# A macaron RWKV-7 block in split fp32: more Strassen-like quads in the down and output projections, and a planner that lists more of the transfers

## The chip, the cores and the metric

One core of a Trainium2 chip runs the whole block; everything below is one launch. The metric is device time in microseconds, the median of three runs: 2014.39 us before the change (2014.39 to 2014.5). The profiled execution, a run of its own, took 2014.53 us; its span, from the first instruction to the last, is 2012.8 us.

## The reference, cut to what matters

All arrays are fp32; 256 tokens, model width 2048, feed-forward width 5632.

```python
def _hybrid_mixer(u, w_in, ...):
    p = u @ w_in
    z_a, z_b, g_a, g_b = jnp.split(p, IN_SPLITS, axis=-1)
    y_a = _rwkv7_branch(z_a, ...) @ w_proj_a      # a scan over the tokens, 16 heads of 64
    y_b = _pool_branch(z_b, pool_w, pool_scale) @ w_proj_b
    m = jax.nn.sigmoid(g_a) * y_a + jax.nn.sigmoid(g_b) * y_b
    return m @ w_out

def reference(x, ...):
    f = _swiglu(_rmsnorm(h, ln_ffn1_pre[l]), ffn1_gate[l], ffn1_up[l], ffn1_down[l])
    h = h + MACARON_WEIGHT * _rmsnorm(f, ln_ffn1_post[l])
    mx = _hybrid_mixer(_rmsnorm(h, ln_mix_pre[l]), ...)
    h = h + _rmsnorm(mx, ln_mix_post[l])
    f = _swiglu(_rmsnorm(h, ln_ffn2_pre[l]), ffn2_gate[l], ffn2_up[l], ffn2_down[l])
    h = h + MACARON_WEIGHT * _rmsnorm(f, ln_ffn2_post[l])
```

## The kernel before

**Splitting.** Every fp32 operand of a matmul is split into a high and a low part of type fp32r, and a product is three matmuls (`mm3`, lines 271 to 275): high by high, low by high, high by low. The high part of a weight is a cast on ACT, the low part a subtraction on DVE (the "low" below). A weight tile holds two blocks of 128 rows by 512 columns. A tile is either one of a small ring (`w32` for the fp32 data, four buffers; `wH`, `wL`, five each) or one of 33 general units (`kH`, `kL`, and in some places `w32`).

**Pairs and quads.** `seven` (line 458) computes two column blocks of 512 at once, called f and l. A letter of its order string is one step. `f` or `l` is a plain pair: two k blocks, two token halves, three matmuls each, so 12 matmuls and one low of 1024 columns. `q` is a quad: two k blocks of both column blocks by seven products instead of eight, so 21 matmuls where an f and an l would need 24. For it DVE makes sums of weights (`t13`, `t24`) and three lows of 1024 and one of 512 columns, and the activations need sums of their own (`sums`, line 381). A capital letter is a pair whose low part is made without DVE (`feed_add`, line 304): ACT writes the negated high part, and an accumulating DMA, issued on POOL, adds the fp32 data.

**Stages.** A feed-forward block runs gate and up in column blocks of 512 (`ffn`, line 847; blocks 2 to 10 by `seven` with the orders of `FAST`), turns the result with DVE transposes and small POOL DMAs (`carry`, line 770), and then runs `post` (line 996): two column pairs of down with the orders of `DOWN`. The mixer's output projection uses `post` with `OUT`: a plain block, one pair by `seven`, a plain block. The last 16 k blocks of the last pair are done one token half after the other (`TRAIL`).

**The order of the work.** In the feed-forward blocks and the projections the PE order is written down in sequence, and every other operation is a job with a duration, a due time and its dependences. `play` (line 168) walks through time and hands out the jobs of ACT (A), DVE (V), POOL (G) and the weight transfers on SP (D), always the ready one with the earliest due time; what comes out is the fixed instruction order of each engine. On the chip nothing is reordered: an engine that waits holds up all that is queued behind it.

**The RWKV chain.** In the mixer PE alone has a written order. `chain(hf)`, for the two halves of the heads, yields the time of matmuls that shall stand between its steps, and `weave` puts that much of other work there (`fill`: the remaining input projections, and last `pair_g`, the first half of `w_proj_a` for two column blocks). `FILL` and `FILB` are two of these times, ahead of the first pA and the first pB of each half. The last steps of a half are the matmuls pY (scan output), pg (gate) and 64 small transposes pT; from pT and pg DVE makes the half's output y in two parts by eight scalar_tensor_tensor operations (lines 1767, 1769), ACT casts the high parts `yH` (1771), and DVE subtracts the low parts `yL` (1772). `w_proj_a` over the second half of y comes right behind in PE's order.

**The head.** SP first loads the transposed x and the first gate weights, then `cols`, then the four row tiles of x (lines 1806 to 1809), from which ACT takes the sums of squares.

## Time and profile before

| | |
|---|---|
| median of three runs | 2014.39 us |
| the profiled execution | 2014.53 us, span 2012.8 us, TensorE clock 0.998 |
| PE busy | 1997.0 us (99%), 9936 matmuls |
| DVE busy | 1764.8 us (88%) |
| ACT, POOL busy | 1200.2 us (60%), 339.8 us (17%) |
| HBM | 202 GB/s over the span |

PE is busy nearly all the time, but a matmul's recorded end is modelled, and the records overlap; what a matmul costs is the distance from start to start. The windows of 50 us say how close the other engines are: DVE is busy between 48.7 and 50.0 of 50 us from 150 to 450 us, in the gate and up blocks of the first feed-forward, 112.68 of 115 us in the first pair of the first down, and much less in the mixer.

### The profile page before, as it was taken

To read this page: it belongs to the slowest core of one execution; us is meant where nothing else is said; L and a number is where in the kernel's file an instruction comes from. 1 tells how busy PE (TensorE), PEld (TensorE's weight loads), DVE (VectorE), ACT (ScalarE), POOL (GpSimd) and SP (SyncE) were. 2 spreads that over 40 slices of the span, in tenths; PEclk is the share of its full clock that TensorE was granted. 3 is DMA by queue.
4 is the path that set the end of the run, shared out by engine and by line. 5 is a ranking of instruction groups with operands and counts; after the bars stand their busy time and mean duration, and the time that the engine had idled before them with its cause. 6 is when DMAs were issued, how large, how long until landed. Compare 5 with 4: busy or idle time off the path is not lost.

```text
span 2012.8 us, 28601 instructions
## 1 busy us (share of the span) xinstructions
PE 1997.0 (99%) x9936; PEld 1651.9 (82%) x9936; DVE 1764.8 (88%) x2362; ACT 1200.2 (60%) x1599; POOL 339.8 (17%) x689
## 2 busy tenths in 40 slices
PE   9999999999999999999999999999999999999997
PEld 7888888888888888888788788888888888888886
DVE  6999999999998857789689678679999999999885
ACT  7556666566655656775575444565556655756553
POOL 0131112211000113403220120002211131110000
PEclk9999999999999999999999999999999999999999
DMA  9777777766667777757466567766777877666674
GB/s 331 235 217 230 230 242 222 236 185 211 216 205 255 238 203 211 211 176 214 141 182 183 160 218 240 254 219 180 220 228 225 256 218 231 195 215 209 206 258 142
DMA packets 230305, 435.09 MB, mean 216 GB/s; under 512 B 25104, under 2 KB 28688, under 8 KB 230160
## 3 DMA queue, kind: packets, MB, share of 16 engines
q1 hardware_dynamic: 205008, 387.18, 59.9%
q0 software_dynamic: 24864, 45.95, 8.4%
q8 instruction: 78, 1.28, 0.3%
q14 instruction: 67, 0.55, 0.1%
q10 hardware_dynamic: 288, 0.14, 0.0%
HBM read 398.79 MB, written 8.39 MB: 202 GB/s over the span
## 4 chain that ended last, share of the span: by engine, by line
PE 97%; DVE 1%; issue 1%; ACT 1%; DMA 0%; SPq 0%; POOL 0%; DVEq 0%; POOLq 0%; ACTq 0%
PE mm L273 27%; PE mm L275 26%; PE mm L274 26%; PE ms L275 5%; PE ms L274 5%; PE ms L273 5%; PE pA L1596 0%; PE tr L750 0%; DMA w<-in_ffn_gate_dram 0%; PE mc L732 0%; DVE fg L1052 0%; PE pU L1692 0%; DVE wL L298 0%; DVE xL L759 0%; PE pSa L1704 0%
## 5 line engine op out<-in xcount | busy, mean ns | idle before, releaser
L273 PE MATMUL mm<-wH,xH 128*128 128x512 f32 (+1 forms) x1711 | 668.8, 391 | 0.0
L274 PE MATMUL mm<-wL,xH 128*128 128x512 f32 (+1 forms) x1711 | 663.2, 388 | 0.8 <-DVE wL L250 0.8
L275 PE MATMUL mm<-wH,xL 128*128 128x512 f32 (+1 forms) x1711 | 663.4, 388 | 0.3 <-DVE xL L759 0.3
L275 PEld LDWEIGHTS mm<-wH,xL 128*128 128x128 f32 x1711 | 321.2, 188 | 66.8 <-DVE xL L759 0.7
L273 PEld LDWEIGHTS mm<-wH,xH 128*128 128x128 f32 x1711 | 321.3, 188 | 66.3 <-ACT wH L249 0.3
L274 PEld LDWEIGHTS mm<-wL,xH 128*128 128x128 f32 x1711 | 321.5, 188 | 64.6 <-DVE wL L250 1.1
L292 ACT CAST wH<-w 128x1024 fp32r<-128x1024 f32 x251 | 262.6, 1054 | 174.8 <-PE mm L275 122.9
L298 DVE TENSOR_TENSOR wL<-w,wH 128x1024 fp32r<-128x1024 f32 x251 | 301.3, 1218 | 58.3 <-ACT wH L292 56.7
L530 ACT CAST wH<-t 128x1024 fp32r<-128x1024 f32 x163 | 171.8, 1054 | 194.5 <-DVE t L515 69.6
L250 DVE TENSOR_TENSOR wL<-w,wH 128x1024 fp32r<-128x1024 f32 (+2 forms) x159 | 188.2, 1192 | 74.4 <-ACT wH L249 73.0
L781 POOL DMA_DIRECT2D x<-T x352 | 173.3, 511 | 434.4 <-DVE T L768 238.0
L249 ACT CAST wH<-w 128x1024 fp32r<-128x1024 f32 (+2 forms) x159 | 162.7, 1027 | 135.6 <-PE mm L275 113.6
L534 DVE TENSOR_TENSOR wL<-t,wH 128x1024 fp32r<-128x1024 f32 x163 | 196.1, 1216 | 17.3 <-ACT wH L530 17.0
L530 ACT CAST wH<-w 128x1024 fp32r<-128x1024 f32 (+1 forms) x161 | 132.9, 826 | 120.7 <-PE mm L275 68.8
L273 PE MATMUL mm<-kH,xH 128*128 128x512 f32 x449 | 175.5, 391 | 0.0
L275 PE MATMUL mm<-kH,xL 128*128 128x512 f32 x449 | 174.9, 389 | 0.0
L274 PE MATMUL mm<-kL,xH 128*128 128x512 f32 x449 | 174.7, 389 | 0.0
L534 DVE TENSOR_TENSOR wL<-w,wH 128x1024 fp32r<-128x1024 f32 (+1 forms) x161 | 151.1, 938 | 1.1 <-ACT wH L530 1.0
L515 DVE TENSOR_TENSOR t<-w,w 128x1024 f32<-128x1024 f32 x104 | 126.5, 1217 | 6.5 <-DMA w<-in_ffn_down_dram 2.7
L298 DVE TENSOR_TENSOR kL<-w,kH 128x1024 fp32r<-128x1024 f32 x95 | 113.6, 1216 | 6.3 <-ACT kH L292 6.0
L292 ACT CAST kH<-w 128x1024 fp32r<-128x1024 f32 x95 | 98.1, 1048 | 19.5 <-DMA w<-in_ffn_gate_dram 9.3
L275 PEld LDWEIGHTS mm<-kH,xL 128*128 128x128 f32 x449 | 84.3, 188 | 18.0 <-DVE xL L759 0.5
(377 smaller groups left out, 2895.6 us busy)
## 6 DMA issues: line engine op xcount, KB each, us to landing
w<-in_w_in_dram SPq DMA_DIRECT2D x128, 512.0 KB, 4.2
w<-in_ffn_down_dram SPq DMA_DIRECT2D x116, 512.0 KB, 4.7
w<-in_ffn_up_dram SPq DMA_DIRECT2D x104, 512.0 KB, 5.0
w<-in_ffn_gate_dram SPq DMA_DIRECT2D x103, 512.0 KB, 6.1
w<-in_ffn_gate_dram SPq DMA_DIRECT2D x146, 256.0 KB, 4.1
w<-in_ffn_up_dram SPq DMA_DIRECT2D x144, 256.0 KB, 4.1
w<-in_ffn_down_dram SPq DMA_DIRECT2D x120, 256.0 KB, 4.2
w<-in_w_out_dram SPq DMA_DIRECT2D x28, 512.0 KB, 5.9
```

Source lines behind the costliest of these rows:

```text
L249: s.nc.scalar.copy(vH, v)
L250: s.nc.vector.tensor_tensor(out=vL, in0=v, in1=vH.bitcast(F32), op=ALU.subtract)
L273: nc.tensor.matmul(ps, aH, bH, start=start, stop=False)
L274: nc.tensor.matmul(ps, aH, bL, start=False, stop=False)
L275: nc.tensor.matmul(ps, aL, bH, start=False, stop=stop)
L292: s.nc.scalar.copy(b["H"][:, :m], b["t"][:, :m])
L298: s.nc.vector.tensor_tensor(out=b["L"][:, :m], in0=b["t"][:, :m], in1=b["H"][:, :m].bitcast(F32), op=ALU.subtract)
L515: V.tensor_tensor(out=v["t13"], in0=v["a"], in1=v["b0"].to_broadcast([P, 2, 512]), op=ALU.subtract)
L530: nc.scalar.copy(x[n_][0], v[n_])
L534: V.tensor_tensor(out=L, in0=v[n_], in1=H.bitcast(F32), op=ALU.subtract)
L781: nc.gpsimd.dma_start(out=x[0][q * 32:q * 32 + 32, i], in_=src[i * 32:i * 32 + 32, q])
```

## The change

The order strings change. The first pair of down gets eight quads instead of seven and one capital `L`; in all four strings the quads are mixed in among the pairs where they stood in rising density before. The output's pair gets four quads instead of two, and three capital letters in front. `FAST` for blocks 2 and 3 gets a second capital letter and another order. `FILL` goes from 19.5 to 20.5 and `FILB` from 5 to 6. The planner's transfer lag goes from 2.4 to 2.8, and `moved` adds empty jobs to its D list for transfers that POOL issues (carries, norm weights, reloads, mixer tiles, spills), so that it plans weights around them. The four row tiles of x move from the head into the planned list, with due times 0, 2, 4, 6. Units that hold fp32 weights are named `uw` instead of `w32`. `silu_in` and `times_in` get forms for blocks 0 and 1 that no order uses here (`SECOND` is empty).

```diff
-FILL = 19.5
-FILB = 5
+FILL = 20.5
+FILB = 6
-LAG = dict(P=0.2, A=0.18, V=0.16, G=0.2, D=2.4, N=0.0)
+LAG = dict(P=0.2, A=0.18, V=0.16, G=0.2, D=2.8, N=0.0)
-DOWN = ((0, "fffffffffqffffqfflqlllqllqllqllqlllll", 0),
+DOWN = ((0, "ffllfLlllqqffllfqfqllqfffffqllqfqfll", 0),
-OUT = ((0, "", 0), (1, "fffffqflqlllll", 0), (3, "", TRAIL))
+OUT = ((0, "", 0), (1, "LFLqqfqqflfl", 0), (3, "", TRAIL))
...
+    def moved(s, dur, due, *deps):
+        for d in deps:
+            s.job("D", dur, lambda: None, due, (d,))
...
         ms = [s.job("G", 0.49, lambda i=i, q=q: move(i, q), t, turned, lag=4.0) for i, q in iq]
+        s.moved(0.15, t, *ms)
...
-                s.job("G", 0.55, lambda: nc.gpsimd.dma_start(
-                    out=hsp[i, h, :, c * 512:c * 512 + 512], in_=ap), t + 9, (node,))
+                s.moved(0.9, t + 9, s.job("G", 0.55, lambda: nc.gpsimd.dma_start(
+                    out=hsp[i, h, :, c * 512:c * 512 + 512], in_=ap), t + 9, (node,)))
...
-                for h in range(2):
-                    for c in range(2):
-                        nc.sync.dma_start(out=xs[h][c], in_=x[0, h * P:h * P + P,
-                                                             c * 1024:c * 1024 + 1024])
...
+                    if c % 2 == 0:
+                        t = ROWS[2 * h + c // 2]
+                        d = s.job("D", 1.75, lambda h=h, c=c // 2: nc.sync.dma_start(
+                            out=xs[h][c], in_=x[0, h * P:h * P + P, c * 1024:c * 1024 + 1024]), t)
```

In the built programs PE has 12 instruction rows fewer, all of them 128x512 matmuls (8328 become 8316).

The longer `FILL` and `FILB` take fill from what stood behind the chain. First PE at the end of the second half's chain, before: pT, then `w_proj_a` over the first half of y (yH_3729, yL_3730), in groups of three matmuls; the fence shows the first two groups and the last, and behind it the first that reads the second half (yH_3731, yL_3732).

```order
L1763 MATMUL pT_4515_11525<-ident_78,R_3716_6723 64x64 x16
L273 MATMUL mm_4516_11548<-wH_4508_11488,yH_3729_6752 128x512
L274 MATMUL mm_4516_11548<-wL_4509_11489,yH_3729_6752 128x512
L275 MATMUL mm_4516_11548<-wH_4508_11488,yL_3730_6753 128x512
L273 MATMUL mm_4513_11498<-wH_4508_11488,yH_3729_6752 128x512
...
L273 MATMUL mm_4516_11548<-wH_4511_11494,yH_3729_6752 128x512
L274 MATMUL mm_4516_11548<-wL_4512_11495,yH_3729_6752 128x512
L275 MATMUL mm_4516_11548<-wH_4511_11494,yL_3730_6753 128x512
L273 MATMUL mm_4503_11442<-wH_7139_11624,yH_3731_6754 128x512
L274 MATMUL mm_4503_11442<-wL_7140_11625,yH_3731_6754 128x512
L275 MATMUL mm_4503_11442<-wH_7139_11624,yL_3732_6755 128x512
```

The same place after the change; the second half of y is yH_3948, yL_3949 there.

```order
L1788 MATMUL pT_4733_11559<-ident_78,R_3933_6738 64x64 x16
L281 MATMUL mm_4731_11517<-wH_4728_11509,yH_3946_6767 128x512
L282 MATMUL mm_4731_11517<-wL_4729_11510,yH_3946_6767 128x512
L283 MATMUL mm_4731_11517<-wH_4728_11509,yL_3947_6768 128x512
L281 MATMUL mm_4715_11428<-wH_7621_11639,yH_3948_6769 128x512
L282 MATMUL mm_4715_11428<-wL_7622_11640,yH_3948_6769 128x512
L283 MATMUL mm_4715_11428<-wH_7621_11639,yL_3949_6770 128x512
L281 MATMUL mm_4716_11432<-wH_7621_11639,yH_3948_6769 128x512
```

Seven groups of three stood between pT and the first use of the second half; one stands there now.

DVE at the same place, before: the lows of the second half's first three weights, then the eight operations on pT and pg with the first yL, then the fourth weight's low (wL_7147, from w32_7133), then the second yL.

```order
L298 TENSOR_TENSOR wL_7142_11628<-w32_7131_11608,wH_7141_11627 128x1024
L298 TENSOR_TENSOR wL_7144_11632<-w32_7132_11610,wH_7143_11631 128x1024
L1767 SCALAR_TENSOR_TENSOR R_3719_6726<-pT_4514_11502,cols_90,R_3719_6726 128x256 x2
L1769 SCALAR_TENSOR_TENSOR R_3719_6726<-R_3719_6726,cols_90,pg_4505_11450 128x256 x2
L1767 SCALAR_TENSOR_TENSOR R_3719_6726<-pT_4515_11525,cols_90,R_3719_6726 128x256 x2
L1769 SCALAR_TENSOR_TENSOR R_3719_6726<-R_3719_6726,cols_90,pg_4506_11459 128x256
L1772 TENSOR_TENSOR yL_3732_6755<-R_3719_6726,yH_3731_6754 128x512
L1769 SCALAR_TENSOR_TENSOR R_3719_6726<-R_3719_6726,cols_90,pg_4506_11459 128x256
L298 TENSOR_TENSOR wL_7147_11650<-w32_7133_11612,wH_7146_11649 128x1024
L1772 TENSOR_TENSOR yL_3732_6755<-R_3719_6726,yH_3731_6754 128x512
```

After, with wL_7628, from w32_7615, as the fourth weight's low:

```order
L306 TENSOR_TENSOR wL_7626_11647<-w32_7614_11625,wH_7625_11646 128x1024
L306 TENSOR_TENSOR wL_7628_11663<-w32_7615_11627,wH_7627_11662 128x1024
L1792 SCALAR_TENSOR_TENSOR R_3936_6741<-pT_4732_11536,cols_90,R_3936_6741 128x256 x2
L1794 SCALAR_TENSOR_TENSOR R_3936_6741<-R_3936_6741,cols_90,pg_4722_11483 128x256 x2
L1792 SCALAR_TENSOR_TENSOR R_3936_6741<-pT_4733_11559,cols_90,R_3936_6741 128x256 x2
L1794 SCALAR_TENSOR_TENSOR R_3936_6741<-R_3936_6741,cols_90,pg_4723_11492 128x256
L1797 TENSOR_TENSOR yL_3949_6770<-R_3936_6741,yH_3948_6769 128x512
L1794 SCALAR_TENSOR_TENSOR R_3936_6741<-R_3936_6741,cols_90,pg_4723_11492 128x256
L306 TENSOR_TENSOR wL_7631_11669<-uw_7616_11629,wH_7630_11668 128x1024
L306 TENSOR_TENSOR kL_7633_11673<-uw_7617_11631,kH_7632_11672 128x1024
L1797 TENSOR_TENSOR yL_3949_6770<-R_3936_6741,yH_3948_6769 128x512
```

The fourth weight's low has moved ahead of the whole y calculation, and two further lows, one before, stand between the two yL. ACT's casts of these weights moved with them.

POOL at the start of the output projection, before: the last mixer tile, the carry of the gated sum, the norm weights, the reload of the residual.

```order
L1339 DMA mb_7156_11680<-msp_6756 128x1024
L781 DMA sga_4305_10300<-T1_7164_11724 32x256 x16
L1011 DMA gb_4626_11571<-in_ln_mix_post_dram 128x1024
L1011 DMA gb_4627_11572<-in_ln_mix_post_dram 128x1024
L1830 DMA h1_2300_426<-hsp_131 128x1024
```

After, with the accumulating DMAs of the three capital letters:

```order
L1364 DMA mb_7636_11692<-msp_6771 128x1024
L789 DMA sga_4522_10315<-T1_7642_11719 32x256 x16
L1034 DMA gb_4863_11586<-in_ln_mix_post_dram 128x1024
L330 DMA wL_7689_11962<-uw_7674_11883 128x1024
L330 DMA wL_7697_12005<-w32_7680_11912 128x1024
L330 DMA kL_7707_12058<-w32_7690_11964 128x1024
L1034 DMA gb_4864_11587<-in_ln_mix_post_dram 128x1024
```

Three transfers are added to this stretch of POOL's queue, behind the carry and one load of norm weights.

More of the change, by code (lines that the diff above doesn't have):

```diff
@@ L864, in f @@
                     sig[h] = get()
[L865 to L866 removed]
+                    nc.scalar.activation(out=sig[h], in_=sig[h], func=AF.Silu, scale=r[h])
+                sj[h] = s.job("A", 0.59, f, t, (*deps, b < 2 and uj[h]))
                 return sj[h]
@@ L1024, in ev @@
                         s.job("N", 0, None, 0, (a,))
-                        s.job("G", 0.0, reload, t, (a,))
+                        g = s.job("G", 2.0, reload, t, (a,))
+                        for i in range(4):
+                            s.moved(1.75, t + 4 * i, g)
                     def some():
```

43 lines of the change are left out of this document (29 added, 14 removed).

## The prediction

> **What bounds the kernel now.** I read the page first (busy time, then the chain that ended last), then PE's waits, then the chain piece by piece at both ends and around the RWKV steps, then windows by stage.
>
> ```profile
> PE 1997.0 (99%) x9936; PEld 1651.9 (82%) x9936; DVE 1764.8 (88%) x2362; ACT 1200.2 (60%) x1599; POOL 339.8 (17%) x689
> PE 97%; DVE 1%; issue 1%; ACT 1%; DMA 0%; SPq 0%; POOL 0%; DVEq 0%; POOLq 0%; ACTq 0%
> ```
>
> The chain runs through PE for 97% of the span. PE's whole list of waits (engine, line, what it waited for, us in total, times, longest):
>
> ```profile
> PE warm L649 <- POOL ident masks.py:199: 1.7, 1, 1.7
> PE mm L274 <- DVE wL L250: 0.8, 1, 0.8
> PE pS L1712 <- ACT R L1706: 0.7, 1, 0.7
> PE mm L275 <- DVE xL L759: 0.3, 1, 0.3
> ```
>
> Without the warm-up that is 1.8 us in the whole run. The matmuls follow each other at the engine's own pace, here in the chain near the end (start, us, what), 20 matmuls between the two rows:
>
> ```profile
> 1984.91 0.23 PE mm L273
> ...
> 1989.44 0.24 PE mm L275
> ```
>
> 4.53 us for 20 is 0.2265 us each. So the kernel is as long as its matmuls, plus some 7 us in front and 11 behind the last one, which the change leaves as they are. A gain comes from fewer matmuls, or from the 1.8 us; a loss comes from any new wait of PE. I looked for those.
>
> **The matmuls.** A quad needs 21 matmuls where two pairs need 24. One more in the first pair of each down, two more in the output's pair: 4 x 3 = 12 fewer, as in the built programs. 12 x 0.2265 = 2.72 us, all on the path. The Trainium skill (TensorE: Matmul & The Clock Gate, Back-to-back issue gap) gives a sustained 131 ns for matmuls of 512 columns beside their weight loads; 12 x 0.131 would be an estimated 1.57 us, and the sum below 2014.6; the trace, with 0.2265, disagrees, and decides.
>
> **DVE in down.** Windows by stage (stretch, length, then PE, PEld, DVE, ACT, POOL busy, clock, DMA share, GB/s): the first pair of the first down, its second pair, the two halves of the output projection, the first pair of the second down; then the DVE groups of the first stretch.
>
> ```profile
> 464.00:579.00 115.00, 115.00 (x509) 95.27 (x508) 112.68 (x143) 69.97 (x89) 8.39 (x17) 1.00 0.66 215
> 579.00:693.00 114.00, 114.00 (x513) 94.46 (x512) 96.44 (x114) 66.81 (x89) 5.48 (x10) 1.00 0.70 230
> 1225.00:1275.00 50.00, 50.00 (x226) 41.53 (x225) 37.68 (x42) 23.79 (x29) 0.54 (x1) 1.00 0.56 176
> 1275.00:1320.00 45.00, 45.00 (x208) 37.27 (x207) 37.05 (x62) 27.99 (x58) 7.13 (x13) 1.00 0.81 276
> 1764.00:1879.00 115.00, 115.00 (x509) 95.27 (x508) 111.48 (x143) 67.03 (x83) 8.39 (x17) 1.00 0.67 216
> ```
> ```profile
> L298 DVE TENSOR_TENSOR wL<-w,wH 128x1024 fp32r<-128x1024 f32 x31 | 37.0, 1219 | 1.0 <-ACT wH L292 0.8
> L519 DVE TENSOR_TENSOR t<-w,t 128x512 f32<-128x512 f32 x8 | 5.5, 683 | 0.0
> L405 DVE TENSOR_TENSOR sf<-x 128x256 f32<-128x256 f32 x4 | 1.7, 418 | 0.0
> ```
>
> A quad costs DVE four operations of 1.219 (t13 and three lows) and three of 0.683: 6.93 us. The first pair of down gains a quad and loses three plain lows (30 before, 27 now): 6.93 - 3.66 = 3.27 us more. DVE has 115 - 112.68 = 2.32 us idle there in the first down, 3.52 in the second, and 17.6 in the pair that follows. The second capital letter in blocks 2 and 3 takes 2 x 1.219 = 2.44 us off DVE before it. I take nothing for it, as the excess, 3.27 - 2.32 = 0.95, is less than that; the bounds are 0 and 0.95 in the first down and 0 in the second. The quads that now stand early in the string shift DVE's work within the stage; below 0 it can't go, since PE has no wait there to lose.
>
> **DVE and POOL in the output's pair.** Plain lows 12 become 5 (8.5 us less), two quads add 13.9, their activation sums four operations of 0.418 and two like 1.219, 4.1: together 9.5 us more, against 12.3 + 7.95 us of DVE idle in the two windows. Nothing. The nine further accumulating DMAs (one in each of blocks 2 and 3 and in down, per feed-forward, and three at the output) land some 7 us after their issue:
>
> ```profile
> kL<-w POOLq DMA_DIRECT2D x9, 512.0 KB, 6.7
> ```
>
> The planner starts them 9 us ahead of use, and none of the 18 of before is in PE's list. I take nothing; if POOL's queue (carry in front) holds one up, the cost is between 0 and one whole landing, 6.7.
>
> **The head and the planner's entries.** The rows of x now start behind three weights on SP instead of ahead of them. Weights come earlier, the row statistics later; they are needed for the gate's evacuation, whose banks PE wants again only after the 96 matmuls of up, 21.7 us later. Nothing. The empty jobs and the lag issue nothing; they only change the order of ACT, DVE, POOL and SP.
>
> **The end of the RWKV chain.** This is where I expect a new wait. Each half of the chain takes some 2 us more fill (1 + 1 by the constants), and for the second half that fill was what hid the calculation of y: seven groups of three matmuls, 4.8 us, stood between pT and the first use of the second half of y; one group, about 0.9 us with the slower first matmul, is left. The first half's end shows how long y takes when DVE is free (chain, then ACT, then DVE by the timeline):
>
> ```profile
> 1013.31 2.01 PE pT L1763 x64
> 1015.32 0.43 PE mm L273
> 1015.75 0.23 PE mm L274
> ```
> ```profile
> 1016.12 0.62 ACT L1771 CAST yH<-R 128x512 fp32r<-128x512 f32 x1 [0.25 <-DVE R L1769]
> ```
> ```profile
> 1014.43 0.88 DVE L1767 SCALAR_TENSOR_TENSOR R<-pT,cols,R 128x256 f32<-128x256 f32 x2 [0.25 <-PE pT L1763]
> ...
> 1017.18 0.68 DVE L1772 TENSOR_TENSOR yL<-R,yH 128x512 fp32r<-128x512 f32 x1
> 1017.79 0.47 DVE L1769 SCALAR_TENSOR_TENSOR R<-R,cols,pg 128x256 f32<-128x256 f32 x1
> 1018.67 1.22 DVE L250 TENSOR_TENSOR wL<-w,wH 128x1024 fp32r<-128x1024 f32 x1 [0.42 <-ACT wH L249]
> 1019.82 0.68 DVE L1772 TENSOR_TENSOR yL<-R,yH 128x512 fp32r<-128x512 f32 x1
> ```
>
> From pT's end at 1015.32 (call it T) yH is done at T + 1.42, the first yL at T + 2.54, the second at T + 5.18, with one low in between. Now: PE has its one group done at T + 0.89 and waits for yH, 0.53 us; two matmuls later, at T + 1.88, it waits for yL until T + 2.54, 0.66 us. The next three groups take it to T + 4.8, and the third matmul of the fifth group, at T + 5.3, needs the second yL. There two lows stand in between instead of one: without the wait of 0.42 that is T + 5.85, with it T + 6.3, so 0.57 to 1.0 us. In all 1.8 us (1.76 to 2.2). Queued behind PE's wait is the rest of `w_proj_a`, which everything later waits for, so it counts in full. The second half's own end in the trace of before says the same: pT ends at 1186.69, and the first yL is done at 1189.74, 3.05 us later.
>
> ```profile
> 1184.68 2.01 PE pT L1763 x64
> ```
> ```profile
> 1189.05 0.69 DVE L1772 TENSOR_TENSOR yL<-R,yH 128x512 fp32r<-128x512 f32 x1
> ```
>
> **The sum.** -2.72 + 1.8 = -0.9 us. From the profiled execution, 2014.53 (span 2012.8), that is 2013.6; the median lies 0.14 lower, so 2013.5. About 0.2%, 4.0 us, is what a measurement of this kernel can tell from no change.
>
> **The rivals.** *The fourth weight is late, and the kernel is slower.* The fourth weight of `w_proj_a`'s second half has its low now ahead of all of y on DVE, and its cast ahead of yH on ACT. In the trace of before ACT waited for just this weight:
>
> ```profile
> 1189.22 1.05 ACT L292 CAST wH<-w 128x1024 fp32r<-128x1024 f32 x1 [0.61 <-DMA w<-in_w_proj_a_dram]
> ```
> ```profile
> 1174.80 5.30 SPq L235 DMA_DIRECT2D w<-in_w_proj_a_dram  x4
> ```
> ```profile
> 1175.06 1.06 POOL L1339 DMA_DIRECT2D mb<-msp  x2 [2.02 <-issue]
> ```
> ```profile
> DMA to landing us min/median/max: 3.7/8.0/11.9
> ```
>
> It landed at 1189.2, T + 2.5, the last of the four issues that began at 1174.80, beside the mixer tiles that POOL loads; landing there took up to 11.9 us where 3.7 is possible (all weights from 1165 to 1215). The Trainium skill has a rule for this (DMA: Bandwidth & Descriptors, Issuing engines are not separate DMA queues): transfers of SP, ACT and POOL run on the same 16 engines and interleave; by it the mixer tiles delay the weight, and the trace agrees. Cast and low take 1.05 + 1.22, and y would otherwise start at T - 0.89, so each us that it lands after T - 3.2 delays PE by one. The change frees its buffer some 5 us sooner, as PE uses up the first half's weights earlier; issued 5 us sooner it lands near T - 2.5 or before, a delay of 0.7 at most, and with a median landing of 8.0 at none. If it stays in the queue behind the mixer tiles, it comes as late as before: 5.7 us more, 2019.2; halfway, 2016.4. The kernel is slower than before from 0.9 us on, that is from a landing at T - 2.3. Chance 0.25, with 2016 as its middle.
>
> *y is hidden anyway*: 2014.39 - 2.72 = 2011.7. For it, DVE's work before pT may be so short that y starts earlier; against it, y can't start before pT, and PE has 0.9 us of work left. Chance 0.17.
>
> *DVE falls behind in down, or an accumulating DMA is late*: 0.95 from the first down, up to 6.7 from one landing, on top of the 1.8: 2014.5 to 2020. The windows speak against the first, the list of waits against the second. Chance 0.09.
>
> *The change doesn't do what it says*: 12 matmuls are gone in any case, but the planner's entries could remove PE's remaining waits, and with y hidden that gives 2014.39 - 2.72 - 1.8 = 2009.9. Of the 1.8, 0.8 is in the head before anything that moved. Chance 0.04.
>
> **How the numbers follow.** The forecast, 2013.5, has 0.45. The range takes in y hidden at its lower end (2011.7, less 0.2 for a lost wait) and the late weight beyond halfway at its upper: 2011.5 to 2017.4; outside are the full lateness, a late DMA and the lost waits, about 0.15 to 0.2. Faster by over 0.2% needs 2010.4 or less: only the last rival, 0.04. Slower by over 0.2% needs 2018.4: the late weight in full, 0.06, a late DMA or several small waits, 0.05: 0.11. The rest, 0.85, is within 0.2%.
>
> **What would show it.** In the changed profile: PE 12 matmuls shorter, the same 0.2265; in PE's waits new entries of about 0.5 on ACT yH, 0.7 and 0.6 on DVE yL, right behind the second pT, and no DMA named in ACT's wait before them. The forecast is wrong if these are missing (then 2011.7), if DVE's first operation on pT starts after pT's end (the late weight), or if PE waits for a low in down or for a `kL` in the output's pair.

## The result, and the profile after

The changed kernel is slower: 2020.33 us median (2018.58 to 2025.64, 7 runs) against 2014.88 for the kernel before (2014.39 to 2015.11, 7 runs); the recorded ratio is 1.0031, with a 95% interval of 1.0021 to 1.0042 (it is not the quotient of the two medians, which is 1.0027). The forecast was 2013.5, its range ended at 2017.4. The profiled execution took 2020.33 us, span 2018.5.

The page's lines on the engines and on the chain, and then PE's whole list of waits (engine, line, what it waited for, us in total, times, longest), of the changed kernel:

```profile
PE 1997.3 (99%) x9924; PEld 1646.4 (82%) x9924; DVE 1775.9 (88%) x2379; ACT 1211.2 (60%) x1617; POOL 349.7 (17%) x698
PE 91%; DVE 4%; DMA 2%; issue 2%; ACT 0%; POOL 0%; SPq 0%; DVEq 0%; POOLq 0%; ACTq 0%
```
```profile
PE warm L657 <- POOL ident masks.py:199: 1.7, 1, 1.7
PE tr L758 <- DVE sga L1377: 1.6, 1, 1.6
PE mm L282 <- DVE wL L258: 1.0, 2, 0.8
PE pU L1717 <- DVE R L1742: 0.8, 1, 0.8
PE mm L281 <- ACT wH L257: 0.7, 1, 0.7
PE mm L283 <- DVE yL L1797: 0.6, 2, 0.4
PE mm L281 <- ACT yH L1796: 0.6, 1, 0.6
PE mm L281 <- DVE u L581: 0.5, 1, 0.5
PE ms L282 <- DVE wL L542: 0.2, 1, 0.2
```

PE runs twelve matmuls less, and yet its busy time has not fallen, so the busy time does not show what was lost. The chain shows it better: DVE and the DMAs hold 6% of it, where PE had 97% before and has 91% now. The waits on yH and yL are the forecast ones; those on sga, on pU, on `u` (a gate operation of the first feed-forward) and on the lows of down (wL, line 542) are not.

**Where the time went.** The instructions that are no 128x512 matmuls (transposes and the small matmuls of the mixer) are the same 1608 in both programs, so the start of the same one can be compared. "Matmuls" is how many more 128x512 matmuls stand ahead of it after the change, and "net" is the difference of the starts less 0.2265 us for each.

| mark on PE | before, us | after, us | matmuls | net, us |
|---|---|---|---|---|
| transposes of the row statistics (head) | 57.71 | 58.30 | 0 | 0.59 |
| first transposes behind the first down | 686.98 | 688.64 | -3 | 2.34 |
| pg of the second half | 1177.82 | 1182.49 | +15 | 1.27 |
| first transposes of the gated sum (sga) | 1207.84 | 1210.52 | -3 | 3.35 |
| their second part | 1219.62 | 1224.02 | -3 | 5.08 |
| last matmul | 2000.16 | 2005.07 | -12 | 7.63 |
| end of the span | 2012.8 | 2018.5 | -12 | 8.4 |

So 8.4 us were lost and 2.7 gained: 0.6 at the head, 1.75 in the first feed-forward with its down, 2.08 at the end of the RWKV chain, 1.73 at the second part of the sga transposes, 2.55 in what follows (nearly all in the second down), 0.7 behind the last matmul; the mixer up to pg gave 1.07 back, for a reason that stays open. Only the third of these had been forecast. The list of waits shows little of what the downs lost: in the second one the largest idle time of PE is 0.18 us, and 2.2 of the 2.55 us are fourteen delays of 0.10 to 0.34 us from one start to the next.

**The end of the chain.** DVE there (start, length, instruction), from the first operation on pT to the second yL:

```profile
1190.48 0.88 DVE L1792 SCALAR_TENSOR_TENSOR R<-pT,cols,R 128x256 f32<-128x256 f32 x2 [0.78 <-PE pT L1788]
...
1193.23 0.69 DVE L1797 TENSOR_TENSOR yL<-R,yH 128x512 fp32r<-128x512 f32 x1
...
1194.22 1.22 DVE L306 TENSOR_TENSOR wL<-uw,wH 128x1024 fp32r<-128x1024 f32 x1
1195.36 1.22 DVE L306 TENSOR_TENSOR kL<-uw,kH 128x1024 fp32r<-128x1024 f32 x1
1196.49 0.69 DVE L1797 TENSOR_TENSOR yL<-R,yH 128x512 fp32r<-128x512 f32 x1
```

DVE's first operation waits 0.78 us for pT itself, so the fourth weight was not late. PE, which has one group of matmuls left, then waits for yH and both yL; the two lows between the yL are those of the order.

**The sga transposes.** DVE at the second part of the gated sum, before and then after:

```profile
1213.77 1.30 DVE L1349 TENSOR_TENSOR sga<-mm,sga 128x512 f32<-128x512 f32 x2
1214.98 0.68 DVE L1352 TENSOR_TENSOR sga<-sga,mb 128x512 f32<-128x512 f32 x1
1218.21 1.29 DVE L807 TENSOR_TENSOR xL<-sga,xH 128x512 fp32r<-128x512 f32 x2 [2.55 <-ACT xH L803]
1219.42 0.69 DVE L1352 TENSOR_TENSOR sga<-sga,mb 128x512 f32<-128x512 f32 x1
```
```profile
1220.78 1.30 DVE L816 TENSOR_TENSOR xL<-sga,xH 128x512 fp32r<-128x512 f32 x2 [3.48 <-ACT xH L812]
1221.99 1.28 DVE L1374 TENSOR_TENSOR sga<-mm,sga 128x512 f32<-128x512 f32 x2
1223.19 1.28 DVE L1377 TENSOR_TENSOR sga<-sga,mb 128x512 f32<-128x512 f32 x2
```

xL is the low of the carried first part; it waits for ACT's xH, and that for the last of the carry's DMAs (landed at 1220.0). Before, three of the four gate operations (those on sga) were done ahead of that wait; now all four are queued behind it, and PE's transposes need the last of them. Already before, there was no slack: the last gate operation began at 1219.42, PE's transposes at 1219.62.

### The profile page after: what moved, and what is told of

Its sections match the earlier page's. It is cut to its first block, busy times and chain, and to the rows that moved or that the text cites. A ratio compares the mean times of both kernels' runs of the same rounds, so it can differ in the third digit from the quotient of the medians.

```text
span 2018.5 us, 28670 instructions
## 1 busy us (share of the span) xinstructions
PE 1997.3 (99%) x9924; PEld 1646.4 (82%) x9924; DVE 1775.9 (88%) x2379; ACT 1211.2 (60%) x1617; POOL 349.7 (17%) x698
## 4 chain that ended last, share of the span: by engine, by line
PE 91%; DVE 4%; DMA 2%; issue 2%; ACT 0%; POOL 0%; SPq 0%; DVEq 0%; POOLq 0%; ACTq 0%
PE mm L281 25%; PE mm L283 24%; PE mm L282 24%; PE ms L282 5%; PE ms L283 5%; PE ms L281 5%; DMA w<-in_ffn_down_dram 1%; DVE wL L542 1%; DVE wL L306 1%; DMA sga<-T 1%; PE tr L758 0%; DVE xL L816 0%; PE pA L1621 0%; DMA uw<-in_ffn_gate_dram 0%; DMA wL<-w 0%
## 5 line engine op out<-in xcount | busy, mean ns | idle before, releaser
L300 ACT CAST wH<-w 128x1024 fp32r<-128x1024 f32 x210 | 219.0, 1053 | 121.9 <-DMA w<-in_ffn_down_dram 49.4
L306 DVE TENSOR_TENSOR wL<-w,wH 128x1024 fp32r<-128x1024 f32 x210 | 252.1, 1220 | 33.9 <-ACT wH L300 32.4
L538 ACT CAST wH<-w 128x512 fp32r<-128x512 f32 (+1 forms) x127 | 106.8, 843 | 76.8 <-PE mm L283 41.5
L281 PE MATMUL mm<-kH,xH 128*128 128x512 f32 x385 | 150.5, 391 | 0.0
L282 PE MATMUL mm<-kL,xH 128*128 128x512 f32 x385 | 149.9, 389 | 0.0
L283 PE MATMUL mm<-kH,xL 128*128 128x512 f32 x385 | 149.9, 389 | 0.0
L542 DVE TENSOR_TENSOR wL<-w,wH 128x512 fp32r<-128x512 f32 (+1 forms) x127 | 122.4, 963 | 4.4 <-ACT wH L538 4.2
L282 PEld LDWEIGHTS mm<-kL,xH 128*128 128x128 f32 x385 | 72.3, 188 | 15.3 <-DVE kL L306 0.4
L281 PEld LDWEIGHTS mm<-kH,xH 128*128 128x128 f32 x385 | 72.3, 188 | 14.8
L523 DVE TENSOR_TENSOR t<-w,w 128x1024 f32<-128x1024 f32 x64 | 78.0, 1219 | 3.6 <-DMA w<-in_ffn_down_dram 3.5
```

What stands on the lines that cost most here:

```text
L281: nc.tensor.matmul(ps, aH, bH, start=start, stop=False)
L282: nc.tensor.matmul(ps, aH, bL, start=False, stop=False)
L283: nc.tensor.matmul(ps, aL, bH, start=False, stop=stop)
L300: s.nc.scalar.copy(b["H"][:, :m], b["t"][:, :m])
L306: s.nc.vector.tensor_tensor(out=b["L"][:, :m], in0=b["t"][:, :m], in1=b["H"][:, :m].bitcast(F32), op=ALU.subtract)
L523: V.tensor_tensor(out=v["t13"], in0=v["a"], in1=v["b0"].to_broadcast([P, 2, 512]), op=ALU.subtract)
```

## The experiments

Seventeen runs: sixteen further kernels, and the kernel before again. The table gives, for the profile of each, the same sums as above: us lost against the first profile of the kernel before, net of matmuls, by stretch. Mixer start is from the transposes behind the first down to pg of the second half, chain end from there to the first sga transposes, sga from these to their second part, end from there to the last matmul (second feed-forward and down), tail what is behind it. A profile is one execution, whose time stands beside the median of all.

| run | matmuls | head | first ffn, down | mixer start | chain end | sga | end | tail | profiled, us | median, us |
|---|---|---|---|---|---|---|---|---|---|---|
| the changed kernel | -12 | 0.6 | 1.75 | -1.1 | 2.08 | 1.73 | 2.55 | 0.73 | 2020.33 | 2020.33 |
| before_again | 0 | 0.1 | 0 | 0 | 0 | 0 | 0.3 | 0 | 2014.93 | 2014.93 |
| fill_alone | 0 | 0.6 | 0.6 | -0.8 | 3.24 | 0 | 0.2 | 0 | 2018.39 | 2017.54 |
| fill_back | -12 | 0.8 | 0.7 | -0.3 | 0 | 0.99 | 2.0 | 0.73 | 2016.98 | 2017.64 |
| no_capital_in_down | -12 | 0.2 | 1.9 | 1.1 | 2.08 | 1.15 | 2.4 | 0.57 | 2021.36 | 2021.36 |
| down_back | -6 | 0.8 | 0.1 | 1.6 | 2.08 | 1.39 | 1.5 | 0.67 | 2021.4 | 2021.82 |
| no_planner_entries | -12 | 0.2 | 2.3 | -0.8 | 3.21 | 0 | 3.7 | 0.74 | 2021.16 | 2021.33 |
| entries_alone | 0 | 0.7 | 0 | 4.0 | 0 | 1.99 | 3.9 | 0 | 2025.1 | 2022.3 |
| out_alone | -6 | -0.1 | 0 | 0 | 0 | 0 | 0.1 | 0.24 | 2013.52 | 2013.69 |
| down_alone | -6 | 0.4 | 1.0 | 3.7 | 0 | 0 | 4.2 | 0.16 | 2022.6 | 2025.66 |
| orders_alone | -12 | 2.6 | 3.6 | 0.5 | 0 | 0 | 3.6 | 0.73 | 2022.85 | 2019.25 |
| capital_alone | 0 | 2.9 | 0.8 | 3.6 | 0 | 0 | 1.7 | 0.16 | 2023.73 | 2023.1 |
| late_eight_and_capital | -12 | 0.6 | 1.0 | 0.2 | 0 | 0 | 3.8 | 0.40 | 2017.77 | 2017.69 |
| early_seven | 0 | 0 | 0 | 3.6 | 0 | 0 | 0.6 | 0 | 2018.66 | 2018.48 |
| early_eight | -6 | -0.1 | 0.6 | 0 | 0 | 0 | 4.2 | 0 | 2017.9 | 2016.29 |
| split_double | -6 | -0.1 | 2.4 | 0.3 | 0 | 0 | 1.1 | 0 | 2016.79 | 2016.29 |
| out_and_late_eight | -12 | 0.1 | 0 | 0 | 0 | 0 | -0.2 | 0.24 | 2012.06 | 2012.65 |
| out_fast_late_eight | -12 | -0.1 | 0 | 0.5 | 0 | 0 | -0.2 | 0.57 | 2012.7 | 2013.06 |

Some cells of the table are chance. The profiles of entries_alone, capital_alone and orders_alone were the slowest of their runs, that of down_alone the fastest, and that of early_eight lies 1.6 us above its median. fill_alone has the order of the kernel before on every engine up to 888 us, and still lost 0.6 at the head and 0.6 in the first feed-forward with its down (a wait of 0.37 us on `u`). So the changed kernel's own wait on `u` (0.48 us, about 0.7 of its 1.75) is not shown to come from the change.

The theory at the outset: the forecast mechanism at the chain's end is right, and something in the downs, in the planner's entries, or both makes the rest.

**FILL and FILB.** The kernel before with them alone, and the changed kernel without them.

```diff
-FILL = 19.5
-FILB = 5
+FILL = 20.5
+FILB = 6
```

> The kernel before, with FILL 20.5 and FILB 6 and nothing else. Theory (the longer fill uses up the matmuls that covered y): the end of the second half of the RWKV chain gets waits of PE on yH and yL of some 1.9 to 2.1 us in sum, as in the changed kernel (2.08 between pg and the first sga transposes there), and the time is 2016.8 (2014.88 + 1.9). Rival (the planner's empty jobs and the other orders make those waits): no such waits, 2014.9. Second rival (the fill pays inside the chain: the pS wait of 0.7 goes and nothing comes): 2014.2.

> The changed kernel with FILL 19.5 and FILB 5 as before. Theory: the waits on yH and yL right behind the second pT go, 2.1 us, and the rest (head, both downs, the sga transposes) stays: 2018.2 against 2020.33. Rival (they come from the planner's entries): 2020.3, waits in place. If the wait of the transposes on sga (1.7) is a consequence of the late chain end, it goes too: 2016.5.

fill_alone: 2017.54 (2016.59 to 2018.78), ratio 1.0012 (1.0003 to 1.0021). fill_back: 2017.64, 2.7 less than the changed kernel. Two rows of PE's waits in fill_alone:

```profile
PE mm L275 <- DVE yL L1772: 1.8, 2, 1.4
PE mm L273 <- ACT yH L1771: 0.6, 1, 0.6
```

In fill_back there is no wait on y at all, and the loss at the chain's end is 0. Both directions agree, so the theory stands and the first rival falls. The second rival had one thing right: in all five kernels with the longer FILL and FILB the wait on pS (0.7) is gone, but one on pU (0.8) has come. That fill_alone loses 3.24 instead of 2.08 is one more low (three, where two stand after the change) between the two yL. The sga wait stayed in fill_back, smaller, so it is not a consequence of the late chain end.

**The planner's entries and the lag.** The changed kernel without them, and then these entries (with the x rows and the names) with all strings, FILL and FILB of before.

```diff
     def moved(s, dur, due, *deps):
-        for d in deps:
-            s.job("D", dur, lambda: None, due, (d,))
+        return
...
-LAG = dict(P=0.2, A=0.18, V=0.16, G=0.2, D=2.8, N=0.0)
+LAG = dict(P=0.2, A=0.18, V=0.16, G=0.2, D=2.4, N=0.0)
```

> The changed kernel with the empty jobs left out (moved does nothing) and the transfer lag back at 2.4; strings, FILL, FILB and x rows stay. On DVE two gate operations stand again ahead of the carry's lows at the last half of w_proj_a, as before. Theory (the empty jobs put xL ahead of sga there, and a late carry then holds up PE's transposes): the wait of the transposes on sga (1.7 us, 1.0 to 1.4 in the other runs) goes, 0.3 at most stays, and the waits on yH and yL stay: 2018.8. Rival (the transposes wait because the chain ends late, whatever the order): the wait stays, 2020.3. Second theory, for the downs (the entries change when weights are issued and so cause DVE's waits there): PE's losses in both downs fall below 0.5 as well, 2016.5.

> The changed kernel with the strings, FILL and FILB of before: only the lag, the empty jobs, the x rows and the names are new; same matmuls as before. Theory (the empty jobs put the carry's lows ahead of the gate operations on DVE): PE's transposes of the gated sum wait 1.0 to 1.7 us for sga, and nothing else comes: 2014.7 + 1.4 = 2016.1. Rival (that wait needs the late chain end as well): no wait there, 2014.7. Second rival (the entries also cost in the downs): 2 us more.

Without the entries: 2021.33 (2021.16 to 2023.63). Three gate operations stand ahead of xL again, and the sga wait is gone, as the theory has it; but a third low stands between the two yL, so that the chain's end lost 3.21 instead of 2.08, and the two feed-forwards with their downs lost 2.3 and 3.7, more than with the entries, so that the second theory did not come true here. The entries alone: 2022.3 (2020.16 to 2025.1), ratio 1.0036 (1.0024 to 1.0049), with the chain's end at 0 and the sga wait there:

```profile
PE tr L758 <- DVE sga L1377: 1.8, 1, 1.8
PE warm L657 <- POOL ident masks.py:199: 1.7, 1, 1.7
PE ms L282 <- DVE wL L542: 1.4, 2, 0.8
PE pA L1621 <- DVE R L1597: 1.3, 2, 1.1
PE pB L1640 <- DVE R L1632: 1.0, 2, 0.8
```

So the entries make the sga wait by themselves. In all five kernels that have them DVE's order has xL ahead of all four gate operations, and in all others three of the four ahead of xL. They cost more than any theory had said: in the profile, the slowest of six, 4.0 at the mixer's start (pA and pB wait for DVE) and 3.9 behind the sga transposes, of which some 1.5 are a slower clock (last section) and the rest waits in the second down, on the old strings. Lag and empty jobs were not tried apart; the x rows stay in no_planner_entries, so they alone do not make the sga wait.

**The strings of down and of the output.** The changed kernel with the old strings of down; the kernel before with the new strings of down alone, of the output alone, and with all new strings.

```diff
 # down_back (and, the other way round, down_alone)
-DOWN = ((0, "ffllfLlllqqffllfqfqllqfffffqllqfqfll", 0),
-        (2, "fflfqllfqqffqffqflfqflqqfflf", TRAIL))
+DOWN = ((0, "fffffffffqffffqfflqlllqllqllqllqlllll", 0),
+        (2, "fffqffqffqffqffqffqflqllqlll", TRAIL))
 # out_alone
-OUT = ((0, "", 0), (1, "fffffqflqlllll", 0), (3, "", TRAIL))
+OUT = ((0, "", 0), (1, "LFLqqfqqflfl", 0), (3, "", TRAIL))
```

orders_alone has both new strings and the new `FAST`.

> The changed kernel with the order strings of down as before (seven quads, rising density, no capital letter): six matmuls more, 1.36 us. Theory (both of S and D): PE's losses in the two downs, 1.75 and 2.6 us net of matmuls, go: 2020.33 - 4.3 + 1.4 = 2017.4. Rival (the losses there come from the feed-forward blocks ahead, the planner's entries or the lag): they stay, 2021.7.

> The kernel before with the new strings of down and nothing else: six matmuls fewer, 1.36 us. Theory D (the eighth quad and the early quads are too much for DVE, which is busy 112.7 of 115 us there): PE loses 1 to 2 us in each down, 2015.2 to 2017.5. Rival (the strings alone fit, and the losses come with the planner's entries or the feed-forward blocks ahead): no loss, 2013.8.

> The kernel before with the new string of the output's pair and nothing else: six matmuls fewer, 1.36 us; DVE is idle for some 20 of 95 us there. Theory: the whole 1.36 us is gained, no wait comes: 2013.8. Rival (the three accumulating DMAs behind the carry come late, or the extra quads' weights do): a wait of PE on kL or wL between the sga and the fg transposes, 2014.9 or more.

> The kernel before with all the new order strings (blocks 2 and 3, down, output) and nothing else: twelve matmuls fewer, 2.72 us; FILL, FILB, lag, planner entries and x rows as before. If the parts simply add up, this is down_alone plus out_alone plus the second capital letter, which takes 2 x 1.22 us off DVE ahead of each down: theory D: PE loses 1 to 1.5 us in each down, 2014.2 to 2015.2. Rival (strings fit, the rest of the change costs): 2012.2, and the change would have been a gain without FILL and the entries.

out_alone: 2013.69 (2013.31 to 2014.06), ratio 0.9995 (0.9986 to 1.0004): within its interval no change, but in the profile the last matmul starts 1.24 us earlier, and no wait is new but one in the head (0.8 on wH, in front of the first mark). down_alone: 2025.66 (2022.6 to 2027.24), ratio 1.0054 (1.0041 to 1.0067): far more than any theory had. Of its losses, 1.0 and 4.2 lie in the feed-forwards with their downs, and 3.7 at the mixer's start, where only the orders of DVE and ACT differ. orders_alone: median 2019.25, where its theory D had 2014.2 to 2015.2; its profile, at 2022.85 the slowest of ten, has 3.6 in each of the two, and 2.6 at the head. down_back: 2021.82; the first down has no loss left, the second keeps 1.5, and entries_alone, which has the same old strings there, loses there too. So the strings of down cost in both downs, and the entries in the second; the output's string costs nothing. The kernel as a whole gained nothing from down_back, as its mixer's start went from -1.1 to 1.6.

The second pair of down has eight quads in both strings; only their places are new. It was not tried alone, but the profiles tell something: in the second down this pair (the 121 us up to the last matmul) loses 0.2 to 2.3 us in each of the six kernels with the new string (0.9 in the changed kernel), and less than 0.1 in all others. In the first down only orders_alone loses more than 0.1 there, 1.0.

**The capital letter in down.** It was taken out of the changed kernel, put alone into the kernel before, and put into a kernel without losses (below).

```diff
 # no_capital_in_down
-DOWN = ((0, "ffllfLlllqqffllfqfqllqfffffqllqfqfll", 0),
+DOWN = ((0, "ffllfllllqqffllfqfqllqfffffqllqfqfll", 0),
 # capital_alone
-DOWN = ((0, "fffffffffqffffqfflqlllqllqllqllqlllll", 0),
+DOWN = ((0, "fffffFfffqffffqfflqlllqllqllqllqlllll", 0),
 # late_eight_and_capital, against out_and_late_eight
-DOWN = ((0, "fffffffffqfffqfflqllqllqllqllqllqlll", 0),
+DOWN = ((0, "fffffFfffqfffqfflqllqllqllqllqllqlll", 0),
```

> The changed kernel with the one capital letter in the first pair of down written small: same matmuls, DVE has one more low of 1.22 us in each down, POOL one accumulating DMA less. Theory S (the capital letter keeps its weight buffer until the accumulating DMA has landed, SP stands behind it, the next weights come late and DVE and ACT idle): DVE's waits in the first 115 us of each down fall from 2.7 and 5.0 us to about 1, PE's losses in the two downs fall from 1.75 and 2.6 us to 0.5 each, 2017.0. Rival D (DVE has too much work there because the quads stand early): PE loses up to 1.2 us more in each down, 2022.7; 2020.3 if DVE's work and the wait cancel.

> The kernel before with one letter changed: the sixth of the first pair of down is a capital F. Same matmuls; DVE has one low of 1.22 us less and POOL one accumulating DMA more in each down. Theory S (the capital's weight buffer is held until its accumulating DMA lands, the queue of weights stands behind it, and DVE later waits some 2 us for a cast): DVE's waits in the first 115 us of the first down rise from 1.7 to 3 or more, and PE loses between 0 and 1 us in each down: 2014.9 to 2016.9. Rival (the capital is a relief for DVE): DVE's waits stay, no loss, 2014.9 or less.

> The kernel with the output's new string and eight late quads (2012.65), and the sixth letter of the first pair of down a capital F. Theory S (the weight behind the capital comes late and DVE waits for its cast): DVE's waits in the first down rise by 1.5 us or more, PE loses 0.8 to 2.5 us in the two downs: 2013.5 to 2015.2. Rival (the loss of the run with the capital alone was all at the head and at the mixer's start, where its order differed): 2012.6; with 1.22 us less work for DVE even the eighth quad is easier.

capital_alone: 2023.1 (2021.87 to 2023.73), ratio 1.0037 (1.0023 to 1.0051). The chain of waits in its first down (start, length, what):

```profile
467.91 6.46 DMA wL<-w
...
475.86 7.79 DMA w<-in_ffn_down_dram
...
483.73 1.06 ACT wH L292
...
484.81 1.24 DVE wL L298
```

and the wait of SP's queue between 464 and 490 us:

```profile
SPq L235 <- DMA wL<-w: 6.2, 1, 6.2
```

The accumulating DMA of the capital letter is issued at 467.9, when DVE and ACT are busy with the last gate operations, and lands at 474.4. Until then its fp32 tile, one of a ring of four, can't be reused; SP stands in front of it for 6.2 us, and all weights behind it wait too. A plain weight that SP could issue only at 475.86 lands at 483.65, DVE makes its low by 486.05, and PE waits 0.50 us. In the kernel without losses (out_and_late_eight) the letter adds 5.0 us (2017.69, 2016.58 to 2018.57, against 2012.65), and against the profile without it 1.0 us are lost in the first feed-forward with its down and 3.9 in the second: theory S holds, but had said 0.8 to 2.5. The changed kernel has the same chain at its own letter:

```profile
466.88 6.40 DMA wL<-w
...
474.78 6.94 DMA w<-in_ffn_down_dram
...
484.16 0.50 PE mm L282
```

This matmul starts 0.29 us late and the next 0.11. Taking the letter out of the changed kernel gained nothing, though (2021.36). DVE's waits in the first pair fell from 2.7 to 1.2 us, but it had a low more, the two downs still lost 1.9 and 2.4, now on lows of quads, and the mixer's start fell into the slower order. So the letter is one cause of two, and its share in the changed kernel is not shown.

**The mixture and the eighth quad.**

```diff
 # early_seven, against before
+DOWN = ((0, "ffllfllllflqffllfqfqllqfffffqllqfqfll", 0),
 # early_eight, against before
+DOWN = ((0, "ffllfllllqqffllfqfqllqfffffqllqfqfll", 0),
 # split_double, against before
+DOWN = ((0, "ffllfllllqffllfqfqllqffffqfqllqfqfll", 0),
 # out_and_late_eight, against before
+DOWN = ((0, "fffffffffqfffqfflqllqllqllqllqllqlll", 0),
+OUT = ((0, "", 0), (1, "LFLqqfqqflfl", 0), (3, "", TRAIL))
 # out_fast_late_eight, against out_and_late_eight
+FAST = {b: "flqFfLqqqfll" if b < 4 else "Ffqffqlqqlll" for b in range(2, 11)}
```

> The kernel before with the first pair of down in the new mixture but with seven quads and no capital letter (the first quad written as f and l, the L as l): same matmuls and the same work of DVE as before, only earlier quads. Theory P (placement: quads that come while DVE still carries the gate and the splits ask it for work before it can have it ready): PE waits on lows of quads in each down, 1 to 3.5 us, 2016 to 2019. Rival W (only the work of the eighth quad and the capital count): no wait, 2014.9.

> The kernel before with the new mixture of eight quads in the first pair of down, its capital letter written small: six matmuls fewer, 1.36 us; DVE's order at the mixer's start is the one of before here. Theory (the eighth quad does not fit when the quads come early, though seven early or eight late do): PE waits on lows of quads, 0.8 to 1.7 us in each down: 2014.7 - 1.36 + 2.5 = 2015.8. Rival (only the capital letter makes the waits of the downs): no wait there, 2013.3.

> The kernel before with the early mixture of eight quads without a capital letter, but with the second of the two quads that stand in a row moved 13 letters back, among the five f: same matmuls as early_eight, six fewer than before. Theory (two quads in a row ask DVE for 13.9 us in 9.5 us of PE, early, when DVE has no lead yet; that one pair makes the waits of the downs): no wait of PE on a quad's low there, 2014.89 - 1.36 = 2013.5. Rival (eight quads in an early mixture are too many, wherever they stand): waits as in early_eight, 0.5 us in the first down and 3 in the second, 2016.3; in between, if the two in a row are a part of it.

> The kernel before with the new string of the output's pair and with eight quads in the first pair of down, but in rising density as before (nine f, then the quads, no capital letter): twelve matmuls fewer, 2.72 us. DVE has 3.27 us more work in the stretch where it was idle for 2.3 to 3.5 us. Theory P (placement is what costs): no wait, 2012.2, faster than both kernels. Rival W (the work of the eighth quad is too much): PE loses the excess or more late in the pair, 1 us or more in each down, 2014.2 or more.

> As the run with the output's string and eight late quads, and with the new string of blocks 2 and 3 (a second capital letter each, 2.44 us less of DVE's work some 200 us ahead of down). If DVE's debt from the feed-forward blocks decides (it is busy 48.7 to 50 of 50 us there), PE's losses in the downs are smaller than in that run: 2012.2. Rival (the blocks' string changes nothing there, or its accumulating DMAs are late): the same time as that run, or up to 2 us more.

early_seven: 2018.48 (2017.89 to 2019.71), ratio 1.0018 (1.0009 to 1.0027), as slow as theory P had it, but not for its reason: neither down has a wait of PE, and all of the loss is the mixer's start but for 0.5 us on sga. Theory P falls in this form. early_eight: 2016.29, ratio 1.0007 (0.9998 to 1.0016), loses 0.6 and 4.2 us (0.5 of the latter a late part of the sga transposes): the early mixture does not carry an eighth quad. By the medians the loss is 2.8 us (2016.29 against 2014.89 less 1.36 for the six matmuls), since the profile was a slow execution. split_double, the same median, 2016.29, moved the waits and did not remove them (2.4 and 1.1 us; 3.0 by the medians), so the two quads in a row were not the whole cause. out_and_late_eight has the eighth quad, in rising density:

```profile
PE warm L649 <- POOL ident masks.py:199: 1.7, 1, 1.7
PE mm L274 <- DVE wL L250: 0.9, 2, 0.7
PE mm L273 <- ACT wH L249: 0.9, 1, 0.9
PE pS L1712 <- ACT R L1706: 0.7, 1, 0.7
PE mm L275 <- DVE xL L759: 0.3, 1, 0.3
```

That is PE's whole list. Its rows on lines 249 and 250 are the head, where the first mark is 0.14 us later than before; pS and xL are as before. It takes 2012.65 (2011.86 to 2013.24), ratio 0.9988 (0.9979 to 0.9997): the twelve matmuls, 2.72 us, come out whole at the last matmul (2.71 earlier), and it is faster than both kernels. The second capital letters of blocks 2 and 3 add nothing to it (2013.06).

DVE's own rows in the first pair of the first down tell why an average had misled. Before, DVE was busy 112.68 of 115 us; here are out_and_late_eight, then split_double (stretch, length, busy PE, PEld, DVE, ACT, POOL), then what DVE waited for in split_double there.

```profile
464.00:579.00 115.00, 115.00 (x509) 95.21 (x508) 113.54 (x146) 71.38 (x92) 8.39 (x17) 1.00 0.65 211
```
```profile
464.00:579.00 115.00, 113.61 (x498) 92.98 (x498) 110.86 (x141) 71.80 (x92) 8.44 (x17) 1.00 0.64 208
```
```profile
DVE wL L298 <- ACT wH L292: 2.0, 3, 1.4
DVE wL L534 <- ACT wH L530: 1.9, 2, 1.0
```

In the good order DVE is busier and PE never waits; in the bad one DVE is less busy because it waits 3.9 us itself. How long DVE is idle does not tell whether an order fits. ACT, whose casts DVE waits for, waits 17.2 us for weights there in split_double and 9.7 in out_and_late_eight; SP's queue, which fetches them, waits for DVE about as long in both (86 us in sum).

**The kernel before, again.**

> The kernel before, unchanged, for a second profile. If the time up to the first transposes of the row statistics (57.71 us in the first profile, 57.6 to 60.6 in the others) differs from the first profile by more than 0.3 us, what the changed kernel shows at its head (0.6) is chance; if it is 57.7 again, the x rows are the likelier cause.

2014.93, span 2013.2: the head differs by 0.1, the first downs not at all, and 0.3 us lie in the second down. Kernels with the same head code as before lost between 0 and 2.9 us there (capital_alone), so chance plays there; the 0.6 of the changed kernel is inside that spread, and the x rows are neither shown to cost nor cleared.

## Why the prediction was wrong

Term by term, the sum had 1.8 us of loss at the end of the RWKV chain and nothing else. The profile has 8.36: 2.08 there, 4.30 in the two feed-forwards with their downs, 1.73 at the sga transposes, 0.73 behind the last matmul, 0.59 at the head, and 1.07 gained at the mixer's start.

*The matmuls*: right. Twelve fewer, at 0.2265 us, and in out_and_late_eight 2.71 of 2.72 us arrive.

*The end of the RWKV chain*: right in mechanism and nearly in size. Starts 0.53, 0.66 and 0.57 to 1.0 us late were forecast. The matmul that waits for yH starts 0.74 late and the two that wait for yL 0.56 and 0.41, 1.7 in sum (the list counts idle time from a matmul's recorded end, and so has 0.58, 0.39 and 0.25). What the forecast lacked is that the matmul behind each of these starts another 0.11 late: 2.08 from mark to mark, against 1.8.

*The late fourth weight*, the main rival: it did not happen. DVE waited for pT, not for the weight.

*DVE in down*: the step that failed, and the largest. It set the eighth quad's 3.27 us of work against 2.32 us of idle time and 2.44 us of relief, and came to nothing, with 0.95 as the bound. The runs show that work was not the measure: eight quads in rising density cost nothing, eight in an early mixture 4.3 us in the two feed-forwards in the profile of early_eight (0.6 + 4.2 - 0.5; 2.8 by the medians) and 3.5 in that of split_double (3.0). The step had noted that the early quads shift DVE's work within the stage, and took nothing for it, on the reason that PE had no wait there to lose. Why the mixture fails is shown only this far: DVE waits for casts, the casts for weights, and the weights for tiles that DVE frees. Which of these begins it was not settled.

*The accumulating DMAs*: half right. None of those in the output came late; no `kL` is in PE's list. But the step asked only who waits for the landing, and not who waits for the tile that the transfer holds. That is SP's queue, 6.2 us; 5.0 us of time in the kernel with only this letter added.

*The planner's entries*: the second step that failed. That the empty jobs and the lag issue nothing and "only change the order" of the engines was true, but the sum took nothing for that order, and the order cost 1.0 to 2.0 us at sga in each of the five profiles with the entries, and at most 0.5 (early_seven, early_eight) without.

*The stretch behind the last matmul*: the prediction left it as it was, at 11 us. It was 12.67 us from the start of the last matmul before and is 13.40 now, 0.73 that the sum did not have (last section).

*The rivals and the range*: "DVE falls behind in down, or an accumulating DMA is late", 2014.5 to 2020, came nearest, at a chance of 0.09; the range left its upper part out. But its price was an excess of work or a late landing, and neither is what happened. Several small waits, which is what came, had been weighed, together with a late DMA, as 0.05.

What stays open: how an edit of down's strings changes DVE's order at the mixer's start, 200 us later. In the twelve kernels of the table in whose order on DVE three operations of line 1582 stand ahead of the two of line 1547 (by the line numbers of before), the mixer's start loses at most 0.5 us; in the six in which only one does (no_capital_in_down, down_back, entries_alone, down_alone, capital_alone, early_seven) it loses 1.1 to 4.0. PE waits for sgb (0.6) in those six and in no other. Eleven of these programs have the FILL of before and no entries. Between the two marks they have the same order on PE, POOL and SP, and on DVE and ACT one of just two orders: the three with the second one lose 3.6 to 3.7 us, the eight with that of before at most 0.5. So the order on DVE and ACT makes this loss; which operation in it does was not tried. In the changed kernel the three stand ahead of the two.

Also open: the second pair's new string alone, and which share of the losses in the changed kernel's downs belongs to the letter, the mixture and the entries.

## What to carry to other kernels

Where an engine has a few per cent of idle time, ask what that idle time waits for before counting it as room: an edit that adds work and delays its supply pays twice. A transfer that reads a tile holds the tile, so price the queue that wants the tile next, not only the reader of the result. Where a planner writes the order, a change of its costs is a change of the program at every stage: compare each engine's order at each place where PE's margin is near zero, and try the parts of a combined change one at a time, since here the output's string with an eighth quad placed late was worth 2 us, and the whole change cost 5.

## What was unexpected in the hardware

A wait at PE can cost more than itself. In entries_alone PE waited 1.83 us for sga, and then the granted clock fell (stretch, length, busy, and the clock third from the end):

```profile
1222.00:1226.00 4.00, 2.42 (x11) 1.69 (x9) 2.99 (x5) 3.04 (x4) 0.00 (x0) 1.00 0.99 368
1226.00:1230.50 4.50, 4.25 (x16) 3.48 (x17) 4.50 (x6) 2.02 (x3) 0.00 (x0) 0.62 0.36 107
1230.50:1240.00 9.50, 9.50 (x44) 7.80 (x43) 7.22 (x10) 4.11 (x4) 0.00 (x0) 1.00 0.61 208
```
```profile
1228.25 0.63 PE L283 MATMUL mm<-wH,yL 128*128 128x512 f32 x1
1228.68 0.63 PE L281 MATMUL mm<-wH,yH 128*128 128x512 f32 x1
1229.11 0.63 PE L282 MATMUL mm<-wL,yH 128*128 128x512 f32 x1
```

The matmuls start 0.43 us apart instead of 0.2265; six such distances (0.2 us each) and a first one of 0.58 cost some 1.5 us. In capital_alone and orders_alone the same happened at the head, behind two waits close together (1.4 and 0.8 us, 1.1 and 0.8 us); in the changed kernel a wait of 1.57 us at the same transposes left the clock at 1.00. The Trainium skill (TensorE: Matmul & The Clock Gate, What's actually happening) has half rate after an idle window of about 3.4 us, with the windows running freely, and full rate again after about as long. The slow stretch agrees: a mean clock of 0.62 over 4.5 us is, by estimate, 3.4 us at half rate (4.5 x 0.38 / 0.5). The idle time of 1.83 us is shorter than such a window, so the trace does not agree on what it takes.

The span behind the start of the last matmul grows with the number of accumulating DMAs in the whole program: 12.67 us with the 18 of before, 12.83 with 20, 12.91 with 21, 13.07 with 23, 13.24 with 25 and 13.40 with the 27 of the changed kernel, 0.08 us for each, though the last one had been issued over 200 us earlier (at 1776 us in the changed kernel). One profile with 25, down_back, has 13.34. What grows is the longest of POOL's three drains at the end of the program, which begins 2.2 us after the last matmul's start: 9.65 us before, 10.39 after the change (lines 1895 and 1920). In these runs POOL's transfers grew in number by the accumulating ones alone, so that they do not tell whether other transfers of POOL would do the same.
